# Modulation columns by row sums on VectorE, and block products in the first gated network

## The chip, the cores and the metric

The kernel runs on one core of a Trainium2 chip. The metric is the device time of one execution in microseconds: 1256.25 us as the median of 3 runs (1255.35 to 1257.07). All arithmetic is on fp32 values; a product of fp32 accuracy is made of three fast matmuls on a high and a low part of each operand (high x high, high x low, low x high).

## The reference

A trunk of two residual layers over 512 tokens of width 1024. Layer 0 mixes tokens with an S5 state-space layer, layer 1 with FoX attention (16 heads of 64, with a forget gate); after each comes a gated convolutional network with 2816 inner channels. So there are four sub-layers, numbered 0 to 3: S5, first gated network, attention, last gated network. Each is modulated by the vector c:

```python
mod = jax.nn.silu(c) @ w + b                     # (1024) @ (1024, 3072)
shift, scale, gate = jnp.split(mod, 3, axis=-1)
hn = rmsnorm(h, g) * (1.0 + scale) + shift
h = h + gate * sublayer(hn)
# gated network
a, b = jnp.split(hn @ w_up, 2, axis=-1)          # w_up (1024, 5632)
a_conv = conv_b + sum(shift_by(a, 2 - i) * conv_w[i] for i in range(3))
f = (jax.nn.silu(a_conv) * b) @ w_down           # w_down (2816, 1024)
```

Each of the four modulations has three thirds (shift, scale, gate) of 1024 outputs; a third needs a 1024 x 1024 weight, 4 MB.

## The kernel before

Activations lie transposed: channels on the 128 partitions, 8 tiles of channels, 512 tokens along the row. The residual is `h`, the normed input of a sub-layer `a_hi` and `a_lo`.

**Products.** `product` goes over output tiles m. For each it loads a weight tile of 512 KB (`raw`, on SP's queue, three buffers, `RAW`), splits it (`put_parts`: ScalarE writes `w_hi`, L241, VectorE the difference `w_lo`, L242; five buffers each, `WB`), runs 3 x 8 matmuls over 512 tokens (L258) into PSUM, and evacuates by a function of the caller: for the residual L324, for the gated network `gated` (convolution L553 to L558, gate L562, split of the result into `ghi` and `glo`). After an evacuation `tick` lets a background generator take one step.

**Gated networks.** An inner tile f of 128 channels is two output tiles of w_up (branch a and branch b); after a group of inner tiles, the product down adds that group's part to the residual. The first network runs in 2 groups of 11 (`GROUPS`), products up and then products down. The last one is called with `plain=(0, 1, 2, 3)`: in it 18 of the 22 inner tiles go through `quarters`. There the 2 x 2 block product of (256 output channels) x (1024 inputs) x (512 tokens) is made with seven half-size products instead of eight: VectorE makes sums of weight blocks (`sums`, L478), both engines split them, TensorE runs seven times 12 matmuls of 256 columns (L506), and ScalarE (L513) and VectorE (L478, `nm_t`) combine the results before `gated`. Sums of the input are made once by `forms_x` during the plain tiles. The last network has four groups (`QGROUPS`); the products down of group q - 1 stand between the inner tiles of group q.

**Modulation.** The thirds of sub-layer 0, and shift and scale of sub-layer 1, are made by TensorE in the S5 layer (`ada_pe`, L181). The other seven thirds (gate of 1, all of 2 and 3) are background work in the first gated network, `ada_units`: each step loads 128 rows of the weight (`ada_raw`, two buffers, SP's queue), and VectorE multiplies them by silu(c) and accumulates (L207, L209). After eight steps TensorE sums over the partitions (L215), ScalarE copies the row (L219), and `ada_columns` turns rows into columns with five small matmuls (L137, L142), writing `par[i]` (and `ga[i]`, the scaled norm weight).

**Attention.** `fox_values` makes the values and the forget logits with 16 PSUM tiles of products (L1282), and the log-forget sums in a chain of small VectorE operations. `fox_heads` then makes the projections of query and key: output tiles in pairs, even m the query of two heads, odd m the key (`project`). Between the k steps of these products `unit` issues the attention steps of the pair before, in the order written out in `ORDER`: scores (L1377), softmax (reduce on VectorE L1389, exponential on ScalarE, normalisation on POOL), transposes (L1407), weighted values (L1424, L1430, L1431). The forget sums `nf` come per pair by a load on SP's queue.

**Order.** Instructions are put on each engine's queue by a planner that goes by program order, readiness and free buffers; `issue_after` and `behind` add edges that keep an instruction behind another one on its engine. Each queue is then worked off in that order, so an instruction that waits holds all behind it. The beginning of the S5 layer is in written order.

## Time and profile before

| | before |
|---|---|
| median of 3 runs | 1256.25 us |
| the profiled execution, its span | 1255.25 us, 1253.5 us |
| granted TensorE clock, mean | 0.995 |
| TensorE busy | 1234.1 us |
| VectorE busy | 898.1 us |
| ScalarE busy | 566.1 us |
| DMA | 183.22 MB, 146 GB/s on the mean |

The page gives, in this order, the busy time of each engine, the span in slices, the DMA queues, the chain of work that ended last, the costliest groups of instructions, and the DMA issues. In a group's row stand line, engine, operation, names of output and inputs, shapes, count; then busy time and mean duration in ns of one; then the engine's idle time before them and what ended it. In the chain and the timeline the first two columns are the start and the length in us. The stages of the span: S5 0 to 263 us, first gated network to 649, values to 698, heads to 863, product out of attention to about 895, last gated network to the end. Operations on one engine overlap a little, so that a sum of durations is somewhat longer than the busy time.

### The profile page before, as it was taken

The page shows a single profiled execution, that of the slowest core. Times are in us where ns is not written, and L with a number is a line of the kernel's source. Part 1 is how long each engine was busy: PE and PEld are TensorE (multiplying, and loading weights), DVE is VectorE, ACT ScalarE, POOL GpSimd, SP SyncE. Part 2 cuts the span into 40 slices and gives each one's busy share as a digit, 9 for nine tenths or more (in the row PEclk, how much of TensorE's full clock was granted, in tenths as well). Part 3 has the DMA queues.
Part 4 walks back from the last instruction along what each step waited for, and adds up shares of the span by engine and source line. Part 5 has one row for each costly group of instructions (what it writes and reads, how often), then busy time and mean ns, then how long its engine had stood idle before and what let it go on. Part 6 is the DMA issues. An engine that isn't in the chain of part 4 may idle for free.

```text
span 1253.5 us, 19344 instructions
## 1 busy us (share of the span) xinstructions
PE 1234.1 (98%) x7464; PEld 1023.1 (82%) x7464; DVE 898.1 (72%) x1610; ACT 566.1 (45%) x1044; POOL 56.7 (5%) x103
## 2 busy tenths in 40 slices
PE   7999999999999999999999999999999999999997
PEld 2566678898878778788799888888989999999987
DVE  7978887478765547665557477765799888887855
ACT  3543455335332233333334456654456545554543
POOL 0000000000000000000000234321000000000000
PEclk9999999999999999999999999999999999999999
DMA  9778667237744736545413433431313332332331
GB/s 366 231 227 260 206 197 256 86 102 227 243 137 147 237 118 219 164 152 169 139 51 102 142 126 127 128 104 42 95 51 111 118 120 83 106 118 88 102 84 68
DMA packets 73067, 183.22 MB, mean 146 GB/s; under 512 B 23079, under 2 KB 25471, under 8 KB 71951
## 3 DMA queue, kind: packets, MB, share of 16 engines
q1 hardware_dynamic: 72687, 181.46, 45.4%
q8 instruction: 59, 0.97, 0.3%
q10 hardware_dynamic: 288, 0.52, 0.1%
q14 instruction: 33, 0.27, 0.1%
HBM read 175.04 MB, written 6.92 MB: 145 GB/s over the span
## 4 chain that ended last, share of the span: by engine, by line
PE 94%; DVE 2%; DMA 1%; ACT 1%; issue 1%; SPq 0%; DVEq 0%; ACTq 0%
PE mmp L258 58%; PE mmp L506 9%; PE mmp L1110 4%; PE aux L506 4%; PE mmp L1282 2%; PE aux L916 2%; PE aux L1424 2%; PE aux L1407 1%; PE mmp L181 1%; PE mmp L1139 1%; PE aux L997 1%; PE aux L1005 1%; PE aux L1377 1%; PE mmp L1050 1%; PE mmp L1080 1%
## 5 line engine op out<-in xcount | busy, mean ns | idle before, releaser
L241 ACT ACTIVATE w_hi<-raw 128x1024 fp32r<-128x1024 f32 (+4 forms) x197 | 181.7, 927 | 262.3 <-PE mmp L258 210.1
L242 DVE TENSOR_TENSOR w_lo<-raw,w_hi 128x1024 fp32r<-128x1024 f32 (+4 forms) x197 | 211.5, 1078 | 95.5 <-ACT w_hi L241 88.6
L258 PE MATMUL mmp<-a_hi,w_hi 128*128 128x512 f32 (+1 forms) x616 | 232.7, 379 | 1.5 <-ACT a_hi L394 1.5
L258 PE MATMUL mmp<-a_hi,w_lo 128*128 128x512 f32 (+1 forms) x616 | 230.2, 374 | 0.0
L258 PE MATMUL mmp<-a_lo,w_hi 128*128 128x512 f32 (+1 forms) x616 | 229.6, 373 | 0.0
L258 PE MATMUL mmp<-ghi,w_hi 128*128 128x512 f32 (+1 forms) x394 | 147.0, 373 | 0.0
L258 PE MATMUL mmp<-glo,w_hi 128*128 128x512 f32 (+1 forms) x394 | 146.4, 372 | 0.0
L258 PE MATMUL mmp<-ghi,w_lo 128*128 128x512 f32 (+1 forms) x394 | 146.2, 371 | 0.0
L258 PEld LDWEIGHTS mmp<-a_hi,w_hi 128*128 128x128 f32 x616 | 115.6, 188 | 24.8 <-issue 2.6
L258 PEld LDWEIGHTS mmp<-a_hi,w_lo 128*128 128x128 f32 x616 | 116.0, 188 | 20.8 <-DVE w_lo L242 0.3
L258 PEld LDWEIGHTS mmp<-a_lo,w_hi 128*128 128x128 f32 x616 | 116.1, 189 | 19.0
L324 DVE SCALAR_TENSOR_TENSOR h<-mmp,par,h 128x512 f32<-128x512 f32 (+1 forms) x74 | 50.0, 678 | 64.0 <-PE mmp L258 63.9
L258 PEld LDWEIGHTS mmp<-ghi,w_lo 128*128 128x128 f32 x394 | 74.3, 188 | 14.1
L258 PEld LDWEIGHTS mmp<-ghi,w_hi 128*128 128x128 f32 x394 | 74.3, 189 | 13.4
L258 PEld LDWEIGHTS mmp<-glo,w_hi 128*128 128x128 f32 x394 | 74.3, 189 | 13.2
L209 DVE SCALAR_TENSOR_TENSOR ada_acc<-ada_raw,sc,ada_acc 128x1024 f32<-128x1024 f32 x49 | 62.8, 1282 | 27.8 <-DMA ada_raw<-in_ada_w 27.5
L506 PE MATMUL mmp<-w_hi 128*128 128x256 f32 x216 | 60.5, 280 | 0.1
L506 PE MATMUL mmp<-w_lo,w_hi 128*128 128x256 f32 x216 | 60.2, 279 | 0.0
L506 PE MATMUL mmp<-w_hi,w_lo 128*128 128x256 f32 x216 | 60.1, 278 | 0.0
L558 ACT ACTIVATE conv<-conv 128x512 f32<-128x512 f32 x44 | 27.6, 631 | 67.0 <-DVE conv L555 66.6
L1110 PE MATMUL mmp<-a_x,raw 128*128 128x512 f32 x112 | 54.8, 627 | 0.0
L241 ACT ACTIVATE w_hi<-sums 128x1024 fp32r<-128x1024 f32 x40 | 42.4, 1059 | 20.1 <-DVE sums L478 8.8
(306 smaller groups left out, 2509.6 us busy)
## 6 DMA issues: line engine op xcount, KB each, us to landing
raw<-in_w_up SPq DMA_DIRECT2D x88, 512.0 KB, 3.4
ada_raw<-in_ada_w SPq DMA_DIRECT2D x56, 512.0 KB, 4.4
raw<-in_ada_w SPq DMA_DIRECT2D x40, 512.0 KB, 6.0
raw<-in_w_down SPq DMA_DIRECT2D x32, 384.0 KB, 3.2
raw<-in_w_down SPq DMA_DIRECT2D x32, 320.0 KB, 3.0
nf<-nfd SPq DMA_DIRECT2D x8, 1152.0 KB, 5.7
raw<-in_fox_qk SPq DMA_DIRECT2D x16, 512.0 KB, 3.7
h<-in_x SPq DMA_DIRECT2D x8, 512.0 KB, 5.4
```

Source lines behind the costliest of these rows:

```text
L181: self.last_mm = nc.tensor.matmul(ps[32 * qq:32 * qq + 32, :], self.sc32[:, k, :], w[:, q * S:(q + 1) * S], start=(step is steps[0]), stop ...
L209: nc.vector.scalar_tensor_tensor(acc, w, self.sc[:, k:k + 1], acc, op0=ALU.mult, op1=ALU.add)
L241: nc.scalar.activation(hi, src, AF.Copy)
L242: nc.vector.tensor_tensor(lo, src, hi.bitcast(F32), ALU.subtract)
L258: self.last_mm = self.nc.tensor.matmul(o, wt, xt[:, cols], start=(k == 0 and n == 0), stop=(k == nk - 1 and n == 2),)
L324: self.nc.vector.scalar_tensor_tensor(self.h[:, m, cols], ps, self.par[i][:, 16 + m:17 + m], self.h[:, m, cols], op0=ALU.mult, op1=ALU.add,)
L506: self.last_mm = nc.tensor.matmul(o, wt[:, k], xt[:, k], start=(first and k == 0 and n == 0), stop=(k == H - 1 and n == 2), skip_group_che ...
L558: nc.scalar.activation(t, t, AF.Silu)
L916: nc.tensor.matmul(ps[g2][:, j, cols], x[rows, a + j, r].rearrange("p c j -> p (c j)"), self.rr[rows, planes, q, :], start=(j == 0 and r = ...
L1110: nc.tensor.matmul(ps, w[m][:, k, :], x[:, k], start=(k == 0), stop=(k == KT - 1))
L1282: self.last_mm = nc.tensor.matmul(ps[q, b][:, :n], xt[:, k, tb], wt, start=(k == 0 and i == 0), stop=(k == KT - 1 and i == 2),)
L1424: nc.tensor.matmul(pv[:, c * P:], self.v[:, hp, k, r].rearrange("p t d -> p (t d)"), pp[:, r, c + 3 * k:NB + 3 * k, :].rearrange("p b t -> ...
```

## The change

1. The weights of the seven background thirds are laid out anew (`ada_t`): a tile is 128 outputs (partitions) by 1024 inputs. One VectorE operation, `tensor_tensor_reduce` with the row silu(c) broadcast to all partitions (`c_row`), makes the product and its sum along the row, and so one column of 128 outputs. Eight of them and one small addition of the bias make a third; no matmul and no ScalarE copy is needed.
2. For `c_row`, silu(c) is stored to DRAM at the start (element by element: the source has 8 elements on each of 128 partitions, the target has them in rows) on SP's queue, and read back 128 times after the S5 layer's main part.
3. The places: the gate of sub-layer 1 during the S5 layer's last products (loads on POOL's queue, two buffers), the three thirds of sub-layer 2 in the first gated network (POOL's queue, one buffer), those of sub-layer 3 in attention (SP's queue, in the ring of the raw weight tiles). Each sum is queued on VectorE behind the last evacuation.
4. The first gated network now runs with `plain=(0, 1, 2, 3, 6, 11, 17)`: the other 15 inner tiles by block products, in five groups (5, 4, 5, 4, 4), and its last four output tiles go by halves of the tokens instead of the last two. Inner tiles below 4 take no background steps.

```diff
-QGROUPS = (6, 5, 6, 5)
+QGROUPS = ((5, 4, 5, 4, 4), (6, 5, 6, 5))
+THIRDS = ((1, 2), (2, 0), (2, 1), (2, 2), (3, 0), (3, 1), (3, 2))
@@ Trunk.__init__
-        self.sc32 = self.const.tile([P, KT, 32], F32, name="sc32")
+        self.scd = self.dram.tile([KT, P], F32, name="scd")
+        nc.sync.dma_start(self.scd.rearrange("k p -> p k"), self.sc)
@@ ada_units, whole
+    def ada_units(self, *thirds, ahead=1, ring=False):
+        nc = self.nc
+        todo = [(i, t, j) for i, t in thirds for j in range(KT)]
+        def load(n):
+            i, t, j = todo[n]
+            src = self.io["ada_t"][THIRDS.index((i, t)), j]
+            if ring:
+                return self.raw([P, D], src)
+            w = self.bgpool.tile([P, D], F32, name="ada_raw", bufs=ahead)
+            nc.gpsimd.dma_start(w, src)
+            return w
+        ws = [load(n) for n in range(ahead)]
+        yield True
+        for n, (i, t, j) in enumerate(todo):
+            if j == 0:
+                sums = self.bgpool.tile([P, KT], F32, name="ada_s", bufs=2)
+            w = ws.pop(0)
+            with self.behind(*self.normed, *self.evac):
+                nc.vector.tensor_tensor_reduce(
+                    w, w, self.c_row, 1.0, 0.0, ALU.mult, ALU.add, sums[:, j:j + 1]
+                )
+            if n + ahead < len(todo):
+                ws.append(load(n + ahead))
+            if j == KT - 1:
+                cols = slice(KT * t, KT * t + KT)
+                nc.vector.tensor_tensor(self.par[i][:, cols], sums, self.ada_b[:, i, cols], ALU.add)
+                if t == 1:
+                    nc.vector.scalar_tensor_tensor(
+                        self.ga[i], self.par[i][:, cols], 1.0, self.norm_g[:, i, :], op0=ALU.add, op1=ALU.mult
+                    )
+            yield True
@@ ffn
-            groups = QGROUPS if plain else GROUPS
+            groups = QGROUPS[l] if plain else GROUPS
-                self.io["w_up"][l], range(2 * fs[0], 2 * fs[-1] + 2), KT, x, gated, ticks=ticks, **k
+                self.io["w_up"][l], range(2 * fs[0], 2 * fs[-1] + 2), KT, x, gated,
+                ticks=0 if plain and fs[0] < 4 else ticks, **k
@@ s5, behind load_x
+        self.c_row = self.mods.enter_context(tc.tile_pool(name="mods", bufs=1, reuse_waits="tile")).tile(
+            [P, D], F32, name="c_row"
+        )
+        nc.sync.dma_start(self.c_row, self.scd.rearrange("k p -> (k p)")[None].to_broadcast([P, D]))
...
+            self.bg = [self.ada_units((1, 2), ahead=2)]
+            self.tick(1)
-            self.product(self.io["s5_w_out"], range(KT), KT, (zhi, zlo), self.add_residual(i), tail=2, after=after)
+            self.product(
+                self.io["s5_w_out"], range(KT), KT, (zhi, zlo), self.add_residual(i), tail=2, after=after, ticks=2
+            )
@@ fox_values: self.evac = [...]; a tick after every second block
+                if b % 2:
+                    self.tick(1)
@@ fox, fox_heads: ticks=1 in the product out and in the projections
@@ build
-        k.bg = [k.ada_units(1, [2])] + [k.ada_units(n, t) for n in (2, 3) for t in ([0, 1], [2])]
-        x = k.ffn(1, 0, x, k.norm_mod(2), ticks=1)
+        k.bg = [k.ada_units(*((2, t) for t in range(3)))]
+        x = k.ffn(1, 0, x, k.norm_mod(2), ticks=1, plain=(0, 1, 2, 3, 6, 11, 17))
         k.done()
+        k.bg = [k.ada_units((3, 1), (3, 0), (3, 2), ring=True)]
```

More of the change, by code (lines that the diff above doesn't have):

```diff
@@ L192, in ada_pe @@
             yield True
-    def ada_units(self, i, thirds):
+    def ada_units(self, *thirds, ahead=1, ring=False):
         nc = self.nc
-        thirds = list(thirds)
-        rows = self.bgpool.tile([P, S], F32, name="ada_rows", bufs=1)
-        n = 0
-        for t in thirds:
-            acc = self.bgpool.tile([P, D], F32, name="ada_acc", bufs=1)
-            for k in range(KT):
-                w = self.bgpool.tile([P, D], F32, name="ada_raw", bufs=2)
-                nc.sync.dma_start(w, self.io["ada_w"][i, k * P:(k + 1) * P, t * D:(t + 1) * D])
-                if k == 0:
-                    with self.tc.issue_after(self.last_lo.ins):
-                        nc.vector.tensor_scalar(acc, w, self.sc[:, 0:1], None, op0=ALU.mult)
-                else:
+        todo = [(i, t, j) for i, t in thirds for j in range(KT)]
[23 more added lines that the diff above has]
+                if t == 1:
@@ L327, in evac @@
             )
+            self.evac = [add.ins]
             if last:
@@ L397, in apply @@
                 )
+            self.normed = [self.last_lo.ins]
         return (self.rms_stats, apply), x
@@ L775, in s5_params @@
         dt = e.exp(ldt, keep("dt"))
+        self.sc32 = pool.tile([P, KT, 32], F32, name="s5_sc32")
         nc.vector.tensor_copy(self.sc32, self.sc[:, :, None].to_broadcast([P, KT, 32]))
@@ L1307, in fox @@
                 self.add_residual(i), head=4, tail=2, after=after,
-                halves=(slice(0, S),), step=self.unit,
+                halves=(slice(0, S),), step=self.unit, ticks=1,
             )
@@ L1450, in build @@
         x = k.fox(2, x, k.norm_mod(3))
+        k.done()
+        k.mods.close()
         if stop == "fox":
```

32 lines of the change are left out of this document (13 added, 19 removed).

## The prediction

> **What bounds the kernel now.** I read the page's busy shares and chain first, then busy time by stage, then the chain inside the two gated networks.
>
> ```profile
> span 1253.5 us, 19344 instructions
> PE 1234.1 (98%) x7464; PEld 1023.1 (82%) x7464; DVE 898.1 (72%) x1610; ACT 566.1 (45%) x1044; POOL 56.7 (5%) x103
> PE 94%; DVE 2%; DMA 1%; ACT 1%; issue 1%; SPq 0%; DVEq 0%; ACTq 0%
> ```
>
> The chain that ended last is 94% TensorE. So TensorE work that disappears is worth its full time, as long as nothing else becomes late. The stages, from windows of busy time (columns: length; PE, PEld, DVE, ACT, POOL busy with instruction counts; clock; DMA share; GB/s): start, second half of the S5 layer, first gated network, attention's values, attention's heads, and the block-product stretch of the last gated network:
>
> ```profile
> 0.00:36.00 36.00, 27.88 (x114) 9.73 (x114) 29.40 (x162) 9.59 (x14) 1.31 (x20) 0.95 0.96 371
> 203.00:263.00 60.00, 60.00 (x301) 50.47 (x300) 34.43 (x50) 21.74 (x32) 0.00 (x0) 1.00 0.40 127
> 263.00:649.00 386.00, 385.05 (x1851) 316.32 (x1851) 240.77 (x315) 134.16 (x189) 0.00 (x0) 1.00 0.54 168
> 649.00:698.00 49.00, 48.55 (x398) 47.99 (x396) 32.40 (x99) 18.33 (x35) 1.07 (x3) 1.00 0.29 87
> 698.00:863.00 165.00, 164.28 (x943) 135.84 (x942) 107.74 (x267) 96.86 (x235) 54.29 (x80) 1.00 0.35 113
> 935.00:1204.00 269.00, 268.86 (x1900) 250.83 (x1900) 227.23 (x335) 144.01 (x223) 0.00 (x0) 1.00 0.34 106
> ```
>
> TensorE has no idle time in the first gated network, and VectorE is 62% busy there. The last row is the pattern that the first network is to take over: TensorE full, VectorE busy 227.2 of 269 us (84%), no TensorE wait. Only the first 36 us belong to another resource: the DMA engines are 96% busy.
>
> **TensorE work that goes.** The chain inside the first gated network by line, then one block-product tile of the last network with the ordinary products beside it:
>
> ```profile
> by line: PE mmp L258 95.5%; PE aux L215 1.8%; PE aux L142 1.2%; PE aux L137 0.4%; PE aux L371 0.4%; PE aux L341 0.4%; ACT a_hi L394 0.1%; DVE nm_h L391 0.1%; issue 0.1%; DVE rs_y L362 0.0%
> 983.85 8.40 PE mmp L258 x36
> 992.26 2.81 PE mmp L506 x24
> ...
> 1002.12 2.10 PE mmp L258 x9
> ```
>
> Modulation: lines 215, 142 and 137 (reduction of the accumulated rows, and their turning into columns) hold 3.4% of 386 us, 13.1 us. The new row sums land as columns, so no matmul replaces these. Gain 13.1.
>
> Block products: an ordinary 512-column matmul takes 8.40/36 = 0.233 us, so an inner tile of 48 takes 11.20. The block tile, seven products of twelve half-width matmuls, runs from 992.26 to 1002.12: 9.86. Fifteen tiles save 15 x 1.34 = 20.1. The products down keep their matmul count (5 groups instead of 2 only cut it differently).
>
> **What VectorE takes on instead.** Rows of the last network's block stretch, the present modulation step, and the closest relative of the new row sum, the attention's reduce with its accumulator read (it reads PSUM and SBUF, the new one two SBUF tiles):
>
> ```profile
> L242 DVE TENSOR_TENSOR w_lo<-sums,w_hi 128x1024 fp32r<-128x1024 f32 x40 | 48.9, 1222 | 3.2 <-ACT w_hi L241 2.7
> L478 DVE TENSOR_TENSOR sums<-raw 128x512 f32<-128x512 f32 x36 | 23.5, 688 | 13.6 <-DMA raw<-in_w_up 13.5
> L478 DVE TENSOR_TENSOR nm_t<-mmp,nm_h 128x256 f32<-128x256 f32 x52 | 20.4, 418 | 1.9 <-PE mmp L506 1.7
> L324 DVE SCALAR_TENSOR_TENSOR h<-mmp,par,h 128x512 f32<-128x512 f32 x22 | 16.5, 749 | 4.2 <-PE mmp L258 4.1
> L242 DVE TENSOR_TENSOR w_lo<-raw,w_hi 128x512 fp32r<-128x512 f32 x18 | 12.3, 685 | 0.0
> L209 DVE SCALAR_TENSOR_TENSOR ada_acc<-ada_raw,sc,ada_acc 128x1024 f32<-128x1024 f32 x49 | 62.8, 1282 | 27.8 <-DMA ada_raw<-in_ada_w 27.5
> L1389 DVE CUSTOM_DVE_ANT_0 s<-mmp,nf 128x512 f32<-128x512 f32 x14 | 9.1, 680 | 0.0
> L1389 DVE DVE_READ_ACCUMULATOR2_ANT mn<- 128x1 f32 x64 | 5.3, 84 | 0.0
> ```
>
> The reduce over 512 costs 0.68, a plain operation 0.69; a plain one over 1024 costs 1.22. So I take 1.22 + 0.08 = 1.30 for a row sum over 1024, against 1.28 for the step it replaces. Bounds: 1.22, and 1.36, twice the reduce over 512.
>
> [...]
>
> Of 56 sums 8 go beside the S5 products (VectorE 34.4 of 60 us, plus 10: hidden by TensorE's work there, as are the extra 0.5 MB of c_row and the POOL loads at 40% DMA), 24 stay in the first network, 24 move into attention.
>
> In the first network the sums run with inner tiles 5 to 16 (ticks: one per product down, two per ordinary up tile): ten block and two ordinary tiles. TensorE: 10 x 9.86 + 2 x 11.20 + 22 products down (14 of 15 matmuls, 8 of 12) 71.4 = 192.4 us. VectorE: at the last network's 84%, 162; minus 2 x 6.3 for the two ordinary tiles (a block tile has 1.9 more splitting, 4 x 0.69 sums and 4 x 0.42 combinations); plus 4 more product evacuations of about 0.75 + 0.7 through the smaller groups, 6; plus 24 x 1.30 = 31. That is 187 of 192. The other stretches have 84% or less. So it fits, barely.
>
> Waits inside it: the load now has one buffer and is issued on POOL's queue, empty here, once the sum before has read it.
>
> ```profile
> DVE ada_acc L209 <- DMA ada_raw<-in_ada_w: 27.5, 17, 3.5
> ada_raw<-in_ada_w SPq DMA_DIRECT2D x56, 512.0 KB, 4.4
> ```
>
> With two buffers VectorE already stood 27.5 us for these loads. With one, the second of two sums in a tile follows 2.8 to 3.5 us after the first while its load takes at least 4.4: 12 such sums could stand 1 to 2 us each, with splits and combinations queued behind them and TensorE behind those. Bounds: nothing (the sum is ordered later) to 12 x 2 = 24 us. SP loses its 56 waiting issues, which helps the weight loads. I take 3 us, nearer to nothing, because the prepared weights run about half a tile ahead of TensorE.
>
> [...] No load of this trace is issued by POOL.
>
> **Attention.** Nothing is added to TensorE. VectorE goes from 107.7 to about 129 of 165 us in the heads, and from 32.4 to 41 of 49 in the values. The question is the order. One pair of projections: TensorE's chain, then VectorE, ScalarE, the transfer's time to landing, and the end of the values:
>
> ```profile
> 773.22 0.65 PE aux L1407 x6
> ...
> 781.61 1.31 PE aux L1424 x8
> ...
> 791.45 0.66 PE aux L1407 x6
> 774.80 0.69 DVE L1332 SCALAR_TENSOR_TENSOR lo<-mmp,hi 128x512 fp32r<-128x512 f32 x1 [0.32 <-ACT hi L1331]
> 775.75 1.34 DVE L242 TENSOR_TENSOR w_lo<-raw,w_hi 128x1024 fp32r<-128x1024 f32 x1 [0.26 <-ACT w_hi L241]
> 774.67 1.05 ACT L241 ACTIVATE w_hi<-raw 128x1024 fp32r<-128x1024 f32 x1
> raw<-in_fox_qk SPq DMA_DIRECT2D x16, 512.0 KB, 3.7
> 686.03 0.34 DVE v L242
> 686.42 11.77 PE mmp L1282 x96
> ```
>
> The modulation tiles share the three raw buffers with the projection weights, on SP's queue. When three of them wait for their sums, the weights after next can be fetched only after the coming evacuation and its sum. From the end of an even product (773.22): evacuation done 775.5, sum 776.8, issue 0.33, transfer 3.7, high part 1.05: 781.9, low part 783.2. The next but one product starts at 781.61 and needs the low part with its third matmul, at 782.1. So about 1 us late in each of 8 heads; after the odd products the interval is longer (781.61 to 791.45, 9.8) and covers it. Bounds: 0 (a weight slot is free earlier) to 3 us for each of 16 products, 48, if the load of nf, on the same queue, and the softmax delay it further. I take 5. In the values, VectorE's evacuation at 686.03 already released TensorE just in time; seven sums ahead of it may push it by one or two: 0 to 3, taken 1.5.
>
> **The start.** The new store of silu(c) is 1024 elements of 4 bytes each, on SP's queue ahead of the modulation weights, while the chain hangs on the DMA engines:
>
> ```profile
> 18.96 6.19 DMA raw<-in_ada_w
> DMA packets 20902, 25.56 MB, mean 222 GB/s; under 512 B 13417, under 2 KB 14872, under 8 KB 20891
> q1 hardware_dynamic: 20891, 25.40, 70.6%
> 1.18 4.23 DMA h<-in_x
> 2.73 0.21 ACT L84 ACTIVATE sc<-first 128x8 f32<-128x8 f32 x1 [0.72 <-DMA first<-in_first]
> ```
>
> The two packet rows are from the S5 stage (60 to 175 us). 371 GB/s at 96% is 386 at full share, so 25.4 MB would fill 66 us; the engines were busy 70.6% of 115 us, 81. The 15 us left, over 13417 small packets, make 1.2 us for 1024. If the store stands ahead of the loads of x on SP, these too wait, from 1.18 until silu ends at 2.94. Bounds 0 and 1.8 + 1.2 = 3.0. I take 1.2: ScalarE has its result only when the loads of x are issued.
>
> **The sum.** The profiled execution took 1255.25 us: -13.1 - 20.1 + 1.2 + 3 + 5 + 1.5 = -22.5, 1232.75; the median of the runs lies 1.0 higher, so 1233.7.
>
> **Rivals.**
> - Everything is hidden: 1256.25 - 33.2 = 1223. For it: the last network shows block tiles without a TensorE wait. Against: VectorE at 187 of 192 us.
> - The first network's sums hold VectorE: 12 to 24 us of standing come through, 1242 to 1255. For it: the 27.5 us of waits with two buffers. Against: TensorE did not feel those.
> [...]
> - The ring in attention starves the projections: each of 16 products starts 2.5 to 3 us late, 40 to 48 us instead of 5: 1269 to 1277, slower. It decides from about 1.7 us per product (27.5 us of other net gain over 16). For it: three buffers for two streams. Against: weights need a buffer only until they are split, and five split buffers stand behind.
>
> **How the numbers follow.** Chances: forecast as summed, 1226 to 1241, 0.52; all hidden, 1220 to 1226, 0.17; VectorE held in the first network 0.14; half rate 0.06; starved ring 0.08; the two lesser effects in attention and the first network together eating just the gain 0.03. Faster by over 0.2% (2.5 us, about what a measurement here can tell) are the first three but for 0.01 at the upper end of the third: 0.82. Within 0.2% lie that 0.01 and the last case, 0.04. Slower are half rate and starved ring, 0.14. The range 1221 to 1254 leaves about 2 in 100 below and 18 above.
>
> **What would show it.** Right: lines 215, 142 and 137 gone from the chain of the first network; that network 351 to 356 us long; the sum at 1.2 to 1.3 us; heads 165 to 172 us; first 36 us at most 2 longer. Wrong: sums over 2 us, ordinary products in attention waiting for w_hi or w_lo, VectorE standing for ada_raw over 20 us with TensorE idle behind it.

## The result and the profile after

The changed kernel takes 1296.13 us (median of 4 runs, 1294.19 to 1296.65) against 1256.35 us of the kernel before beside it: a ratio of 1.0319, 95% interval 1.0301 to 1.0336. It is 3.2% slower; 1233.7 was forecast. Its profiled execution has a span of 1294.9 us, 41.4 more than before. The page after, busy times and the chain by engine:

```profile
span 1294.9 us, 20598 instructions
PE 1230.7 (95%) x7908; PEld 1042.4 (81%) x7908; DVE 1008.2 (78%) x1871; ACT 611.9 (47%) x1136; POOL 86.3 (7%) x135
PE 62%; issue 14%; DMA 9%; DVE 9%; ACT 5%; POOL 0%; SPq 0%; DVEq 0%; ACTq 0%; POOLq 0%
```

TensorE held 94% of the chain before; now it holds 62%. Loads, VectorE and ScalarE stand between its products. Where, the windows by stage show (columns as in the prediction): start, second half of the S5 layer, first gated network, values, heads, block stretch of the last network and the rest:

```profile
0.00:46.60 46.60, 35.12 (x145) 14.41 (x145) 34.33 (x176) 12.94 (x20) 1.31 (x20) 0.98 0.90 291
...
193.28:271.00 77.72, 77.53 (x382) 65.15 (x383) 53.07 (x76) 31.39 (x42) 3.69 (x7) 1.00 0.61 214
271.00:638.80 367.80, 359.53 (x2294) 325.22 (x2293) 310.53 (x498) 175.58 (x277) 12.13 (x23) 0.99 0.39 130
638.80:705.00 66.20, 53.98 (x396) 52.98 (x395) 35.86 (x112) 16.29 (x35) 1.08 (x3) 0.85 0.21 72
705.00:905.00 200.00, 176.94 (x949) 139.53 (x948) 133.67 (x312) 103.08 (x240) 66.84 (x80) 0.97 0.44 151
...
945.50:1294.90 349.40, 341.68 (x2328) 314.94 (x2328) 285.68 (x442) 181.98 (x287) 0.00 (x0) 0.99 0.29 94
```

Read the length beside TensorE's busy time: in the values 12 us and in the heads 23 us are idle, in the first network 8, and in each of these stretches the granted clock (third number from the end) is below 1.

To compare many kernels the text below cuts each profile at four events: the first conv activation on ScalarE, the first and the last matmul of the values, and the last head's output. The five stretches between are called start (it includes all of the S5 layer), network, values, heads, last part. A stretch is read from one profile of each kernel; the medians come from the runs. In us:

| kernel | start | network | values | heads | last part | median, ratio to before [95%] |
|---|---|---|---|---|---|---|
| before | 286.6 | 362.8 | 48.5 | 165.1 | 390.5 | 1256.35 |
| after | 294.1 | 344.8 | 66.4 | 199.0 | 390.6 | 1296.13, 1.0319 [1.0301, 1.0336] |
| e1 | 292.2 | 350.3 | 63.8 | 198.3 | 390.1 | 1296.5, one run |
| e2 | 297.8 | 348.3 | 48.1 | 168.8 | 390.2 | 1254.9, one run |
| e3 | 295.6 | 347.4 | 64.5 | 198.9 | 391.3 | 1299.5, one run |
| e4 | 290.6 | 349.2 | 66.4 | 201.0 | 390.5 | 1298.1, 1.0330 [1.0308, 1.0352] |
| e5 | 296.5 | 340.8 | 64.4 | 199.9 | 390.2 | 1293.5, one run |
| e6 | 297.2 | 339.8 | 66.4 | 198.7 | 391.1 | 1295.0, one run |
| e7 | 295.1 | 347.2 | 49.3 | 178.8 | 407.4 | 1278.7, 1.0163 [1.0122, 1.0203] |
| e8 | 295.4 | 346.5 | 65.7 | 200.0 | 390.5 | 1299.9, one run |
| e9 | 297.1 | 342.6 | 48.3 | 176.5 | 390.2 | 1256.9, 1.0004 [0.9988, 1.0020] |
| e10 | 298.7 | 363.1 | 48.5 | 165.1 | 390.5 | 1267.2, 1.0085 [1.0068, 1.0101] |
| e11 | 299.0 | 348.2 | 48.1 | 177.4 | 390.2 | 1264.7, one run |
| e12 | 286.4 | 347.0 | 66.1 | 200.4 | 390.4 | 1293.5, 1.0297 [1.0272, 1.0322] |
| e13 | 296.4 | 354.3 | 48.4 | 165.1 | 390.3 | 1256.0, 0.9998 [0.9979, 1.0016] |
| e14 | 291.4 | 352.0 | 48.1 | 165.3 | 390.2 | 1244.1, 0.9902 [0.9885, 0.9918] |
| e15 | 286.1 | 361.0 | 48.4 | 165.0 | 390.2 | 1254.8, 0.9990 [0.9976, 1.0003] |
| e16 | 289.5 | 345.0 | 50.1 | 164.6 | 390.3 | 1241.7, 0.9886 [0.9872, 0.9901] |
| e17 | 293.1 | 378.4 | 49.1 | 165.2 | 390.3 | 1278.0, 1.0176 [1.0159, 1.0193] |
| e18 | 290.7 | 345.3 | 50.5 | 165.2 | 390.3 | 1242.5, 0.9889 [0.9864, 0.9914] |

A stretch scatters from profile to profile: the network with the very code of the changed kernel took 344.8, 350.3, 348.3, 349.2, 347.2 and 347.0 us (after, e1, e2, e4, e7, e12; mean 347.8). Values, heads and last part repeat to about 2 us. From before to after: start +7.5, network -18.0, values +17.9, heads +33.9, last part +0.1; together 41.4.

**Attention.** Waits of TensorE in values and heads after (engine, line waited for; us, times, longest), then the chain through one head:

```profile
PE mmp L1304 <- ACT w_hi L250: 12.1, 2, 6.1
PE mmp L267 <- DVE w_lo L251: 10.8, 6, 1.8
PE mmp L267 <- ACT w_hi L250: 10.7, 7, 5.6
```

```profile
775.52 1.71 ACT s L1421 x7
...
777.28 2.70 ACT s L1421 x8
779.98 0.49 ACT hi L1356
...
780.49 0.69 DVE lo L1357
781.18 1.33 DVE raw L220
...
782.55 4.59 DMA raw<-in_fox_qk
...
787.16 1.07 ACT w_hi L250
...
788.27 0.73 PE mmp L267 x2
```

TensorE ended this even product at 776.7 us. Its evacuation (hi, lo) waits on ScalarE behind 15 exponentials (s, L1421) and is done at 781.2; the modulation sum (raw, L220) waits for the evacuation; the load of weights waits for the sum, because the modulation tile holds the ring's buffer; the split waits for the load, the product for the split. The same loop comes again 21.2 us later (802.42 for the sum), where a head took 18.2 before. The seven waits for w_hi are those of even products, at their start; the six for w_lo are those of odd products, at their third matmul (five of them 1.8 us long); the split w_lo stands there on VectorE behind the softmax's reduces (L1417).

**The sums.** By shape, the sum over a tile from POOL's queue, over a tile from the ring, and the read of the accumulator:

```profile
L220 DVE CUSTOM_DVE_ANT_0 ada_raw<-ada_raw,c_row 128x1024 f32<-128x1024 f32 x32 | 39.0, 1221 | 16.0 <-DMA ada_raw<-in_ada_t 16.0
L220 DVE CUSTOM_DVE_ANT_0 raw<-raw,c_row 128x1024 f32<-128x1024 f32 x24 | 30.6, 1275 | 0.0
L220 DVE DVE_READ_ACCUMULATOR2_ANT ada_s<- 128x1 f32 x56 | 4.5, 81 | 0.0
```

1.22 to 1.28 us and 0.08 for the read: no longer than the plain operations over 1024 in the rows of before (1.22 and 1.28). The trace lists the sum as CUSTOM_DVE_ANT_0, like the attention's reduce over 512 (0.67 us).

### The profile page after: what moved, and what is told of

Read it like the earlier page. It is cut to its first block, busy times and chain, and to the rows that moved or that the text cites. A ratio compares the mean times of both kernels' runs of the same rounds, so it can differ in the third digit from the quotient of the medians.

```text
span 1294.9 us, 20598 instructions
## 1 busy us (share of the span) xinstructions
PE 1230.7 (95%) x7908; PEld 1042.4 (81%) x7908; DVE 1008.2 (78%) x1871; ACT 611.9 (47%) x1136; POOL 86.3 (7%) x135
## 4 chain that ended last, share of the span: by engine, by line
PE 62%; issue 14%; DMA 9%; DVE 9%; ACT 5%; POOL 0%; SPq 0%; DVEq 0%; ACTq 0%; POOLq 0%
PE mmp L267 25%; PE mmp L517 13%; PE aux L517 5%; PE mmp L1123 4%; PE mmp L1304 3%; DMA raw<-in_fox_qk 3%; ACT s L1421 2%; PE aux L929 2%; PE mmp L1152 2%; DMA raw<-in_w_up 2%; ACT w_hi L250 2%; DVE w_lo L251 2%; PE mmp L185 1%; PE aux L1018 1%; PE aux L1010 1%
## 5 line engine op out<-in xcount | busy, mean ns | idle before, releaser
L251 DVE TENSOR_TENSOR w_lo<-raw,w_hi 128x1024 fp32r<-128x1024 f32 (+4 forms) x205 | 201.0, 984 | 53.6 <-ACT w_hi L250 47.8
L267 PE MATMUL mmp<-a_hi,w_hi 128*128 128x512 f32 (+1 forms) x376 | 141.3, 378 | 12.3 <-ACT w_hi L250 10.7
L267 PE MATMUL mmp<-a_hi,w_lo 128*128 128x512 f32 (+1 forms) x376 | 139.3, 371 | 10.9 <-DVE w_lo L251 10.8
L267 PE MATMUL mmp<-a_lo,w_hi 128*128 128x512 f32 (+1 forms) x376 | 137.7, 367 | 0.0
L517 PE MATMUL mmp<-w_hi 128*128 128x256 f32 x396 | 111.2, 281 | 3.6 <-ACT nm_h L524 3.6
L517 PE MATMUL mmp<-w_lo,w_hi 128*128 128x256 f32 x396 | 110.4, 279 | 0.0
L517 PE MATMUL mmp<-w_hi,w_lo 128*128 128x256 f32 x396 | 110.1, 278 | 0.0
L251 DVE TENSOR_TENSOR w_lo<-sums,w_hi 128x1024 fp32r<-128x1024 f32 x74 | 90.2, 1220 | 4.8 <-ACT w_hi L250 4.1
L267 PEld LDWEIGHTS mmp<-a_hi,w_hi 128*128 128x128 f32 x376 | 71.5, 191 | 26.6 <-ACT w_hi L250 12.7
L267 PEld LDWEIGHTS mmp<-a_hi,w_lo 128*128 128x128 f32 x376 | 71.6, 190 | 25.6 <-DVE w_lo L251 14.4
L267 PEld LDWEIGHTS mmp<-ghi,w_hi 128*128 128x128 f32 x388 | 74.4, 192 | 13.1
L517 PEld LDWEIGHTS mmp<-w_hi 128*128 128x128 f32 x396 | 75.1, 190 | 4.6 <-ACT nm_h L524 4.6
L517 PE MATMUL mmp<-a_hi,w_hi 128*128 128x256 f32 x264 | 74.5, 282 | 1.9 <-ACT nm_h L524 1.9
```

The lines of the kernel that those rows point to most:

```text
L251: return nc.vector.tensor_tensor(lo, src, hi.bitcast(F32), ALU.subtract)
L267: self.last_mm = self.nc.tensor.matmul(o, wt, xt[:, cols], start=(k == 0 and n == 0), stop=(k == nk - 1 and n == 2),)
L517: self.last_mm = nc.tensor.matmul(o, wt[:, k], xt[:, k], start=(first and k == 0 and n == 0), stop=(k == H - 1 and n == 2), skip_group_che ...
```

## The experiments

The theory after the result: attention is slow because a modulation tile holds one of the ring's three buffers until its sum; the rival is that VectorE's 31 us of sums, ahead of softmax and splits, are what is late.

**e1: loads without sums.**

```diff
+    n_ = 1 if ring else D
-    w, w, self.c_row, 1.0, 0.0, ALU.mult, ALU.add, sums[:, j:j + 1]
+    w[:, :n_], w[:, :n_], self.c_row[:, :n_], 1.0, 0.0, ALU.mult, ALU.add, sums[:, j:j + 1]
```

> The sums in attention run over one column instead of 1024 (so par of the last network is not the reference's); their 512 KB loads stay in the ring of three raw buffers, with the same release points. In the changed kernel the values take 66.2 us and the heads 200.0 (48.5 and 166.0 before). Theory ring: the buffer that a modulation tile holds until its sum delays the projection weights; only the sum's own 1.3 us leave the loop, so the heads stay at 180 to 196 us, the values at 60 to 66. Rival VectorE: the sums' 31 us ahead of the softmax and the splits are what is late; heads 165 to 170, values 48 to 51.

**e2: sums without loads.**

```diff
     if ring:
-        return self.raw([P, D], src)
+        return self.c_row
...
-    w, w, self.c_row, 1.0, 0.0, ALU.mult, ALU.add, sums[:, j:j + 1]
+    w, w, self.ones[:, 0:1].to_broadcast([P, D]) if ring else self.c_row, 1.0, 0.0, ...
```

> The opposite: no modulation tile is loaded in attention, and the 24 reductions over 1024 columns read the row of silu(c) and a one instead (so par of the last network is not the reference's). VectorE's time stays, the ring has only weights in it. Theory ring: heads 165 to 172 us, values 48 to 52, whole kernel about 1242 to 1250. Rival VectorE: heads over 185, values over 60, whole kernel over 1275.

Values and heads of e1, then of e2:

```profile
642.50:706.30 63.80, 52.78 (x397) 51.78 (x396) 30.63 (x111) 16.40 (x36) 1.08 (x3) 0.89 0.24 75
706.30:904.60 198.30, 177.32 (x945) 138.25 (x944) 112.78 (x311) 102.40 (x239) 61.02 (x80) 0.97 0.46 152
```

```profile
646.10:694.20 48.10, 48.06 (x398) 47.85 (x396) 39.65 (x115) 20.21 (x40) 1.07 (x3) 1.00 0.28 88
694.20:863.00 168.80, 166.42 (x945) 137.06 (x944) 129.34 (x307) 97.26 (x235) 58.10 (x80) 0.99 0.33 110
```

In e1 VectorE has nearly its old load (112.8 us in the heads) and the heads stay at 198.3. In e2 VectorE has all the sums (129.3), no tile lies in the ring, values and heads are 48.1 and 168.8, and no wait of TensorE for weights is left. It is the tiles in the ring, then, and not VectorE's work; that it is not merely their traffic is shown by e7. e1's heads are slower than expected (180 to 196): its chain at 821.9 to 831.8 us is the same loop, exponentials, evacuation, sum, load, and the load takes 5.95 us there where it took 4.59 above. The sums' own price in the heads is at most the 3.7 us that e2 keeps.

**e3: the first network without the sums' VectorE time** (the edit of e1, for the thirds of sub-layer 2).

> In the first gated network alone the 24 sums run over one column (so par of attention is not the reference's); loads and order stay. The changed kernel's first network takes 367.8 us, TensorE idle 8.3 of it. Theory VectorE: VectorE at 310 of 368 us is locally over its time, and what TensorE waits for are splits behind sums; the network then takes 350 to 357 us with TensorE idle under 3. Rival: the block tiles' order of loads and the four tiles of the tail make the gaps; 363 to 368 us, the idle time as before.

347.4 us, no gain, though VectorE has 26 us less to do. It spent the time waiting for the loads of the single buffer, 28.1 us against 13.4 in the changed kernel (shown at e6):

```profile
DVE ada_raw L221 <- DMA ada_raw<-in_ada_t: 28.1, 14, 4.0
```

So VectorE's work was not it.

**e4: silu(c) stored as rows.**

```diff
-        nc.sync.dma_start(self.scd.rearrange("k p -> p k"), self.sc)
+        row = self.tmp.tile([KT, P], F32, name="c_kp", tag="nm_h", bufs=4)
+        nc.gpsimd.dma_start(row, self.io["c_kp"])
+        nc.scalar.activation(row, row, AF.Silu)
+        nc.gpsimd.dma_start(self.scd, row)
```

> The store of silu(c) element by element is gone: a second copy of c is loaded as 8 rows of 128, run through the same function on ScalarE, and stored as 8 packets of 512 bytes, both on POOL's queue. Theory store: the 1024 small packets and SP's wait for silu cost the start about 5 us and what follows 2 more; the start is back at 41.7 to 42.5 us (46.6 in the changed kernel), the whole kernel at 1288 to 1291. Rival: the start is longer for another reason (the later queue order, the moved copy into sc32): it stays above 45 us, the whole kernel at 1295 to 1297.

A miss: the start is 3.5 us shorter, not 5 to 7, and the whole no faster (1295.6 to 1300.7). Beside the means found later (at e12), 290.6 is the level of kernels without a store, so the start did come back; network and heads of this profile were 4.4 and 2.0 us longer.

**e5: the first network's sums without loads** (the edit of e2, for the thirds of sub-layer 2).

> In the first gated network the 24 sums keep their length on VectorE but load nothing: they read the row of silu(c) and a one (so par of attention is not the reference's). From the first conv activation to the forget gate's first operation the changed kernel takes 373.0 us, the one without the sums' VectorE time 375.6. Theory load wait: VectorE stands for a single-buffered load of 5.7 us per cycle, and the preparation of the next block tile is queued behind; without loads this stretch takes 360 to 366 us and TensorE waits for nm_h under 2 us. Rival: the block tiles' own order makes the gaps: 371 us or more, waits for nm_h over 5 us.

**e6: sums spread.**

```diff
                         self.quarters(pool, l, f, x, gated)
+                    if f >= 4:
+                        self.tick(ticks)
                     if q:
                         down(q - 1, range(j * KT // n, (j + 1) * KT // n))
+                        self.tick(ticks)
```

(and no step after each single product)

> First gated network: instead of two sums 3 us apart after two products down, one sum after the products down and one after the inner tile, so the interval between sums is longer than the load. Theory load wait: VectorE's waits for ada_raw fall from 13 us to under 6, the stretch from 373 to 362 to 369 us. Rival (block tiles' own order): no change, 371 us or more.

Waits in the first network after, of TensorE and of VectorE:

```profile
PE mmp L517 <- ACT nm_h L524: 5.5, 6, 1.9
PE aux L351 <- DVE ssq L327: 2.0, 1, 2.0
```

```profile
DVE ada_raw L220 <- DMA ada_raw<-in_ada_t: 13.4, 13, 2.4
```

nm_h is the copy that a block tile makes between its products. Without loads (e5) TensorE's waits for it fall to 0.8 us and the network to 340.8, 7.0 under the mean of the six; spread (e6), to 2.4 us and 339.8. By the stretch that the expectation named, first conv activation to forget gate, e5 took 369.0 us and e6 367.9 (373.0 in the changed kernel): e6 is within what was expected, though VectorE's waits for its loads fell only to 8.7 us and not under 6; e5 gained less than expected. By one profile each, against a mean whose profiles lie between 344.8 and 350.3, the single load buffer accounts for 7 to 8 us of the network, not for all that is missing.

**e7: sums in mid-product.**

```diff
-                if b % 2:
-                    self.tick(1)
...
+        for m in range(NH):
+            self.units.setdefault(KT * m + MID, []).append(lambda n=1 + (m % 5 == 0): self.tick(n))
```

> Attention: no sum in the values; in the heads each sum is called in the middle of a product (at its fifth of eight steps) and not after its evacuation, so that the ring's buffer comes free half a product earlier. Ring theory (it is the time of release that counts, not that a tile is in the ring): values 48 to 52 us, heads 168 to 182 us, whole kernel 1250 to 1272 us. Rival: two streams in three buffers starve the weights wherever the sum stands: heads 190 us or more, whole kernel 1275 to 1290.

Values 49.3 and heads 178.8, as the ring theory said: the time of release counts. The values hold no modulation tile here; the heads, whose row follows, move more than in the changed kernel (163 GB/s on the mean, 151 there), so traffic alone is not what they lost to:

```profile
691.60:870.40 178.80, 169.65 (x944) 135.84 (x943) 128.50 (x310) 99.30 (x235) 58.02 (x80) 1.00 0.49 163
```

But five sums were left for the output product, each again after an evacuation, and the last part lost 16.8 us; TensorE's longest wait there in e7:

```profile
PE mmp L268 <- ACT w_hi L251: 9.6, 1, 9.6
```

So the whole is 1278.7, above the range of the ring theory and inside the rival's, though the heads are well under the rival's 190.

**e8: the last two, not four, output tiles in halves** (`tail=TAIL if plain and l else 2`).

> The first network's last products down are again two in halves at its end, not four. Theory tail: the four held products push the values' weight loads together and TensorE waits 2 us for the squares' sum, then runs at a granted clock of 0.5 to 0.73; with two, this wait goes and the stretch from the first conv activation to the forget gate falls by 2 to 5 us, to 368 to 372. Rival: the end is late because of VectorE's queue and loads before it; no change within 1.5 us.

346.5 us against a mean of 347.8, and 374.2 for the stretch named: no effect.

**e9: the sums rehoused.** Rows as in e4, spreading as in e6, the steps of e7 for 8 sums only:

```diff
-            self.bg = [self.ada_units((1, 2), ahead=2)]
+            self.bg = [self.ada_units((1, 2), (2, 0), ahead=2)]
...
-        k.bg = [k.ada_units(*((2, t) for t in range(3)))]
+        k.bg = [k.ada_units((2, 1), (2, 2), (3, 1), (3, 0))]
...
-        k.bg = [k.ada_units((3, 1), (3, 0), (3, 2), ring=True)]
+        k.bg = [k.ada_units((3, 2), ring=True)]
```

> All 56 sums placed where a buffer is to spare: 16 in the second half of the S5 layer, 32 spread in the first network as in e6 (one after the products down, one after the inner tile), 8 in attention, each in the middle of every second product, none in the values and none in the output product; silu(c) stored as rows as in e4. Stages of before: 286.6, 362.8, 48.5, 165.1, 390.5. If the ring is what attention lost to, the heads fall to 167 to 174 us, the values to 48 to 50, the last part to 390 to 392; the network at 338 to 347, the start at 286 to 292; whole kernel 1232 to 1249, faster than before. Rival (32 sums with one load buffer are too many beside block tiles, or attention loses to any modulation tile in the ring): network over 352 or heads over 178, whole kernel over 1253.

1256.9, no gain on the kernel before and above what was expected. The network came as expected (342.6); the start, 297.1 with 16 sums in the S5 layer's second half, and the heads, 176.5 with only 8 sums, did not. At the end of the S5 layer TensorE waits 3.1 us for the last square, which it did not in the changed kernel. In the heads its own waits are for no weights but, 4.5 us of them, for normalised scores (s, from POOL), though weight loads still hold 24% of the chain there. Why 8 sums in mid-product still cost 11.4 us, when 19 cost 13.7 (e7), stays open.

**e10: the store alone, in the kernel before.**

```diff
+        self.scd = self.dram.tile([KT, P], F32, name="scd")
+        nc.sync.dma_start(self.scd.rearrange("k p -> p k"), self.sc)
```

> The kernel before with one thing added: the store of silu(c), 1024 elements of 4 bytes on SP's queue (nothing reads it). Theory store: it costs by itself 4 to 7.5 us, whole kernel 1260 to 1264, the stretch up to the first conv activation 291 to 294 us instead of 286.6. Rival: the start's length comes from where sc32 and the rest now lie; the store alone costs under 2 us, 1256 to 1258.

10.9 us for 4 KB, more than expected. The first 20 us, of the kernel before, of e10, and of e12 (below):

```profile
0.00:10.00 10.00, 3.89 (x5) 1.65 (x6) 6.71 (x46) 5.29 (x7) 1.31 (x20) 1.00 0.77 277
10.00:20.00 10.00, 9.10 (x42) 2.85 (x42) 7.51 (x71) 3.52 (x6) 0.00 (x0) 1.00 1.03 403
```

```profile
0.00:10.00 10.00, 3.77 (x5) 1.65 (x6) 6.69 (x45) 5.26 (x7) 1.31 (x20) 1.00 0.88 200
10.00:20.00 10.00, 5.82 (x11) 2.15 (x10) 4.20 (x35) 2.74 (x5) 0.00 (x0) 0.81 1.04 181
```

```profile
0.00:10.00 10.00, 4.24 (x5) 1.80 (x6) 6.69 (x45) 5.49 (x7) 1.31 (x20) 1.00 0.76 263
10.00:20.00 10.00, 9.31 (x40) 2.99 (x38) 6.81 (x64) 3.33 (x6) 0.00 (x0) 1.00 1.04 396
```

The last two columns: with the store the DMA engines are as busy as before (104%) and move less than half (181 instead of 403 GB/s). 77 GB/s over 10 us and 222 over 10 more are 3.0 MB, or 7.4 us at 403 GB/s. The packets in the traces say where the time goes: those of 4 bytes are booked at 0.009 us each, but the 2 KB packets of x that start from 8 us on, once the small ones are out, take 0.35 to 1.03 us on the mean (in steps of 2 us) instead of 0.09. The store lands 13.5 us after its issue, and SP, whose next loads stand behind it, waits 4.9 us for that. The other 3.5 us of the 10.9 are not accounted for; TensorE's clock, 0.81 here and 1.00 before in the second 10 us, is a candidate.

**e11: as e9 without block tiles.**

> As e9, but the first gated network has only ordinary inner tiles, so TensorE's gain of 20.1 us from block tiles is gone and VectorE has room. If the block tiles bring what their matmuls save, the network is 349 to 352 us (362.8 less 13.1 for the modulation matmuls), 8 to 12 us longer than in e9. Rival: the block tiles' VectorE work costs what they save; the network is no longer than in e9 by more than 3 us.

Network 348.2, 14.6 us under before: the modulation matmuls' 13.1 and a little. The fifteen block tiles bring another 5.6 (342.6), between the two expectations.

**e12: the row by TensorE, no store.**

```diff
-        nc.sync.dma_start(self.c_row, self.scd.rearrange("k p -> (k p)")[None].to_broadcast([P, D]))
+        for q in range(2):
+            ps = self.aux.tile([P, S], F32, name="aux")
+            for b in range(NB):
+                nc.tensor.matmul(ps[:, b * P:(b + 1) * P],
+                    self.sc[:, NB * q + b:NB * q + b + 1].to_broadcast([P, P]), self.ident, ...)
+            nc.scalar.activation(self.c_row[:, q * S:(q + 1) * S], ps, AF.Copy)
```

> The changed kernel without any store of silu(c): its row is made after the S5 scan by eight TensorE products with the identity (0.27 us each by the like of the norm's rows) and two copies on ScalarE. The store alone, in the kernel before, cost 10.9 us; the version stored as rows still kept 2.3 to 4 us of it. Theory store: the first 20 us are back at 277 to 403 GB/s, the first conv activation at 288 to 291 us (286.6 before, 294.1 in the changed kernel), the whole kernel 3 to 8 us under the changed kernel's 1296.1. Rival: part of the start's loss has another cause (the moved sc32, later loads); it stays at 292 us or more.

The rates are back (fence above) and the start is 286.4. Over more profiles: 286.1 to 293.1, mean 289.5, in the six kernels without the store (e12, e14 to e18), 292.2 to 297.8, mean 295.5, in the eight with it and the same work in the S5 layer (after, e1 to e3, e5 to e8). So the store, with its read-back, costs 6 us there; a further 2.9 over the one profile of before isn't explained, nor why the same store cost 10.9 us in e10. The median gains 2.7 us, just under what was expected.

**e13: none in attention.** e12's row, 16 sums in the S5 layer's second half, 40 in the network.

> Row of silu(c) by TensorE as in e12; 16 sums in the second half of the S5 layer (most of them before its output product's last tiles), 40 in the first network spread over products down and inner tiles, none in attention. If attention lost only to modulation tiles in its ring, values and heads are those of before, 48.5 and 165.1; start 288 to 294, network 342 to 350 (342.6 with 32 sums, 339.8 with 24), last part 390.5; whole kernel 1237 to 1251, faster than before. Rival: VectorE and its single load buffer carry no more in the first network: over 355 us, whole kernel over 1254.

Values 48.4 and heads 165.1: exactly before, so attention's whole loss comes from the modulation work there. The network at 354.3 with 40 sums and the start at 296.4 with 16 in the S5 layer give the gain away (1256.0): both above what was expected.

**e14: 48 sums in the first network, no block tiles**, 8 in the S5 layer, row by TensorE.

> Row of silu(c) by TensorE (start 286.4 in e12), 8 sums in the second half of the S5 layer as in the changed kernel, 48 in the first network, which keeps ordinary inner tiles; none in attention. Theory of four separate prices (store, single load buffer beside block tiles, ring in attention, crowded S5 half): start 286 to 288, network 347 to 351 (348.2 with 32 sums in e11), values 48.5, heads 165.1, last 390.4; whole kernel 1237 to 1244. Rival: 48 loads of 512 KB through one buffer do not fit 350 us without TensorE waiting, or the start comes back to over 292; over 1249.

1244.1 us, faster than both kernels, at the upper end of what was expected; start (291.4) and network (352.0) lie above their ranges. The profiled execution was the slowest of its runs (span 1247.0), with one wait of 2.4 us in the network.

**e15: as e14 with nine block tiles** (`plain=(0, 1, 2, 3, *range(5, FT, 2))`).

> As e14, but every second inner tile from the fifth on is of seven block products, nine in all. Matmul time by the rows of e9 and e11: an ordinary tile 48 x 0.230 = 11.0 us, a block tile 84 x 0.117 = 9.9, so nine save 10.6 at most. If VectorE and the loads keep up (some 80% busy), network 338 to 344, whole kernel 1229 to 1238. Rival: what e9 and e13 lost (waits for the load buffer with the block tile's preparation queued behind, then a slower granted clock) eats it; network 347 or more, no faster than e14.

361.0 us and 1254.8: the rival. Nine block tiles made the network 9 us longer than none.

**e16: as e15 with two load buffers.**

```diff
-QGROUPS = ((5, 4, 5, 4, 4), (6, 5, 6, 5))
+QGROUPS = ((4, 4, 4, 4, 3, 3), (6, 5, 6, 5))
...
-        k.bg = [k.ada_units(*((2, t) for t in range(3)), (3, 1), (3, 0), (3, 2))]
+        k.bg = [k.ada_units(*((2, t) for t in range(3)), (3, 1), (3, 0), (3, 2), ahead=2)]
```

> As e15 (nine block tiles, 48 sums), with two load buffers for the sums in place of one; the room comes from cutting the first network into six groups (4, 4, 4, 4, 3, 3) in place of five, which adds eight products' evacuations on VectorE. Theory single buffer: in e15 VectorE stood 54.6 us for modulation loads and TensorE 14 us behind it; with two buffers the stands fall under 20 us, the network to 340 to 348 us (361.0 in e15), the whole kernel to 1233 to 1243. Rival: VectorE's own time and the order of its queue hold the block tiles' preparation back, whatever the loads do: network 355 or more, whole kernel 1250 to 1256.

The network of e15 with VectorE's waits for its loads and TensorE's for the copy, then the same of e16 with TensorE's longest wait:

```profile
286.10:647.10 361.00, 347.06 (x1896) 300.26 (x1895) 284.60 (x440) 146.37 (x222) 24.91 (x47) 0.98 0.50 164
```

```profile
DVE ada_raw L218 <- DMA ada_raw<-in_ada_t: 51.5, 33, 3.2
```

```profile
PE mmp L515 <- ACT nm_h L522: 7.1, 5, 4.3
```

```profile
289.50:634.50 345.00, 341.14 (x1891) 296.20 (x1890) 292.15 (x456) 151.60 (x230) 25.10 (x48) 0.99 0.53 170
```

```profile
DVE ada_raw L218 <- DMA ada_raw<-in_ada_t: 2.8, 5, 1.3
```

```profile
PE aux L379 <- DVE rs_y L370: 3.1, 1, 3.1
```

With one load buffer more (4 KB on each partition) VectorE's waits for its loads fall from 51.5 to 2.8 us, TensorE waits only at the network's end, and 16 us are gone, although VectorE has more to do (292.2 instead of 284.6 us). The six groups, cut to make the room, changed with it and were not tried alone. At 1241.7 us this is the fastest kernel of the study, 1.1% under the kernel before.

**e17: the same with fifteen block tiles.**

> The same with the changed kernel's fifteen block tiles. VectorE has some 290 us of old work and 62 of sums in 340, so it cannot hide all: by either theory network 345 to 357 us, whole kernel 1238 to 1251; theory single buffer expects it under e13's 354.3 with 40 sums, the rival at or over it.

378.4, above the 345 to 357 that was expected by either theory, and on the rival's side. TensorE waits 25 us for split weights:

```profile
PE mmp L515 <- ACT w_hi L248: 11.4, 5, 3.8
PE aux L515 <- DVE w_lo L249: 9.3, 2, 5.6
PE mmp L515 <- DVE w_lo L249: 4.3, 6, 1.3
```

VectorE is busy 323.7 us of the 378.4, but it also waits 25.7 us for high parts from ScalarE and 13.1 for loads, so it is not shown that its work alone is the bound. Fifteen tiles and 48 sums do not fit in this order; nine tiles do.

**e18: e16 with the tail of two.**

> e16 with the first network's last products down in two halves, not four. In e16 TensorE has no wait in the network but one of 3.1 us (with 0.8 before it) at its end, and a granted clock of 0.74 in those 20 us. If four held products cause it, the network falls from 345.0 to 337 to 342 us and the kernel to 1234 to 1239; if the chain of the norm at the end is late for another reason, as e8 found in the changed kernel, the network stays at 344 or more and the kernel within 2 us of 1241.7.

345.3 and 1242.5: the four held products are not the cause of the wait at the network's end. The chain there (in e16) goes through VectorE's norm steps with other VectorE work between them, a split of 1.12 us among it; moving that was not tried.

## Why the prediction was wrong

The sum had the change at -22.5 us; the profiled executions differ by +41.4. Of the 64 between them, attention makes 45, the network 12 and the start 6.

- **Modulation matmuls, -13.1: right.** e11, with ordinary tiles, gained 14.6 in the network, by one profile.
- **Block products, -20.1: mis-sized, and not all collected.** The changed kernel's chain has 96 ordinary matmuls in one piece, 0.230 us each and not 0.233; an ordinary tile is then 11.04 us, and fifteen save 17.7. Beside the sums they brought 5.6 (e9 against e11).

```profile
210.69 22.08 PE mmp L267 x96
```

- **Eight sums in the S5 layer, nothing: right**; its second half took 77.7 us in both kernels. Sixteen there were too many (e9, e13).
- **Row sum, 1.30 us: right** (1.22 to 1.28 and 0.08). The half rate that the chances give 0.06, a sum of some 2 x 1.22 us, was the author's assumption; the changed kernel's 56 sums took 1.22 us (32 of them) and 1.28 us (24) on the mean, and none shows it.
- **24 sums in the first network, VectorE 187 of 192, +3: the mechanism was named, the size wrong.** VectorE's waits for a single-buffered load came (13.4 us), within the bounds 0 to 24; they cost TensorE 7 to 8 us (e5, e6). The busy-time balance (187 of 192) was the wrong test: taking the sums' work from VectorE changed nothing (e3), and with two buffers and nine tiles TensorE's waits inside the network were gone (e16). The network ended 18 us under before in the changed kernel's profile, 15 on the mean of the six, instead of 30. Of these 15, 7 to 8 are here, 2.4 in the tile's price, and about 5 in the wait of 2.0 us at the network's end and the slower clock behind it (below); that last part no experiment took away (e8). The modulation loads landed 4.0 us after their issue from POOL's queue and 4.1 us from SP's, though the two groups stand in different stages (KB each and median us to landing):

```profile
ada_raw<-in_ada_t POOLq DMA_DIRECT2D x32, 512.0 KB, 4.0
raw<-in_ada_t SPq DMA_DIRECT2D x24, 512.0 KB, 4.1
```

- **The start, 1.2, bounds 0 and 3.0: failed.** It was 7.5 in the changed kernel's profile, 6 by means over profiles, and 10.9 alone (e10). The step that failed priced the store by the engine time of its own packets, taken from a stage in which the DMA engines have slack (busy 70.6%) and averaged over 13417 packets of up to 512 bytes. That time is indeed small, about 0.6 us (1024 x 0.009 over 16 engines, e10). What the store cost was the loads beside it: the 2 KB packets of x took up to ten times as long, and SP waited 4.9 us for the store to land (e10).
- **Attention, 5 + 1.5: failed, and this decided the sign.** +33.9 and +17.9. The starved ring was among the rivals, at 40 to 48 us in the heads and 0.08; it came, at 33.9 in the heads, and in the values too. Three steps failed. First, "evacuation done 775.5", 2.3 us after the product, was read from the kernel before, where nothing hung on it; in the loop the evacuation comes behind ScalarE's exponentials, 4.5 us after the product, and the load behind it takes 4.6 us instead of 3.7. Second, the interval after the odd products was said to cover the delay: six odd products waited for w_lo, as seven even ones did for w_hi. Third, the values were priced by VectorE's order alone, though the same ring feeds them: two waits, 12.1 us together.
- **What was not in the sum at all: the clock.** Some of TensorE's waits cost more than their length. In the values the clock at 0.68 and 0.65 over the 10 us behind the two waits (below) is worth 6.7 us (3.2 and 3.5); with the waits' 12.1 that is 18.8, about the loss of 17.9. In the heads the waits for weights are 21.5 us and a clock of 0.97 over 199 us at most 6; some 6 us of the 33.9 are not accounted for.

One of the forecast's signs of failure was the right one: "ordinary products in attention waiting for w_hi or w_lo" is what the trace shows.

## What to carry over

When a new stream shares a ring of buffers, follow one buffer round: what releases it, what that waits for on each queue, and the load behind it; if the ring closes through an evacuation, the price is a whole load and split per turn (4.59 and 1.07 us in the head shown above), however idle the engines are on average. A background operation on an in-order engine needs its input early, not only a free slot in its busy time: in the changed network taking the sums' loads away was worth 7 us (e5) and taking their work away nothing (e3), and with twice the sums one more load buffer came with a gain of 16 us (e16). Price a scattered store, where the DMA engines are full, at the bandwidth that it takes away there (181 GB/s instead of 403 in the second 10 us of e10), and look for a way without it, as eight small matmuls did here.

## What the runs showed of the hardware

**The clock after a short wait.** The end of the changed kernel's first network, where TensorE waited 2.0 us for the last square, in steps of 2 us:

```profile
626.00:628.00 2.00, 0.78 (x7) 0.57 (x5) 1.54 (x4) 0.91 (x3) 0.00 (x0) 1.00 0.72 252
628.00:630.00 2.00, 1.18 (x5) 1.19 (x6) 0.82 (x2) 0.72 (x2) 0.00 (x0) 0.67 0.02 4
630.00:632.00 2.00, 2.00 (x11) 2.00 (x11) 0.00 (x0) 0.00 (x0) 0.00 (x0) 0.50 0.00 0
...
634.00:636.00 2.00, 2.00 (x13) 2.00 (x13) 0.95 (x5) 0.06 (x1) 0.00 (x0) 0.63 0.00 0
636.00:638.00 2.00, 2.00 (x18) 1.89 (x17) 1.43 (x8) 0.42 (x1) 0.00 (x0) 1.00 0.00 0
```

The granted clock is 0.50 for 6.8 us after it (628.7 to 635.5) and then 1.00 again, so the wait of 2 us cost some 3.4 more. In the values it costs about as much behind each of the two waits of 6 us for weights:

```profile
670.00:680.00 10.00, 9.96 (x58) 9.67 (x59) 6.80 (x21) 1.06 (x1) 0.31 (x1) 0.68 0.32 116
690.00:700.00 10.00, 9.06 (x52) 8.76 (x53) 2.45 (x2) 1.91 (x2) 0.00 (x0) 0.65 0.40 140
```

Not every wait of about 2 us does so: of six waits of 1.8 to 1.9 us in the changed kernel's network and heads, five left the clock at 1.00, and one (from 864.4 us) was followed by a clock of 0.50 for 3.4 us.

**A scattered store.** While the store of 1024 elements of 4 bytes was under way (13.5 us from issue to landing), the 16 DMA engines were 88% to 104% busy and moved 181 to 200 GB/s over 20 us (e10), where they otherwise moved 277 to 403; the 4-byte packets themselves are booked at 0.009 us, the 2 KB loads beside them at up to 1.03 us instead of 0.09. In the changed kernel, whose start has the same store, it landed after 12.7 us, and the 2 KB packets that start from 8 us on took 0.35 to 0.75 us on the mean (in steps of 2 us).
